# Attention finish with one normalizer tile for four query tiles and one broadcast scaling; the filler's merges queued at once

## The chip, the cores and the metric

The kernel runs on one core of one Trainium2 chip. Five kinds of work are told apart in its profile: TensorE's matmuls (PE) and weight loads (PEld), VectorE (DVE), ScalarE (ACT), GpSimd (POOL), and SyncE (SP), which issues all DMAs. The metric is the device time of one execution in microseconds. Three runs of the kernel before have a median of 1716.93 us (1715.32 to 1719.83).

## The reference, cut to what matters

One layer over 1024 latent tokens of width 1024 and 256 context tokens: a modulated RMS norm, one wide input projection, and two branches on the same input, a gated linear attention and a differential attention. The second one is what the change touches. It has 8 heads; each head's queries and keys come as two components of 64.

```python
def one_block(qs):
    qb1, qb2 = qs
    s1 = jnp.einsum('bhqd,bhkd->bhqk', qb1, k1).astype(jnp.float32) * scale
    s2 = jnp.einsum('bhqd,bhkd->bhqk', qb2, k2).astype(jnp.float32) * scale
    a = jax.nn.softmax(s1, axis=-1) - lam * jax.nn.softmax(s2, axis=-1)
    return jnp.einsum('bhqk,bhkv->bhqv', a.astype(v.dtype), v)
...
b = merge_heads(rms_norm(o_diff) * diff_gain * (1 - lam_init)) * jax.nn.silu(diff_gate)
y = jax.nn.sigmoid(m_gla) * (a @ w_br_gla) + jax.nn.sigmoid(m_diff) * (b @ w_br_diff)
return y @ w_out
```

The output of a head is normalized by its own root mean square. That is why the kernel never divides by the softmax's sum: it forms E0 - lam (z0/z1) E1, where E are the exponentials and z their row sums, and corrects in the norm, whose epsilon is then multiplied by z0 squared: (mean of squares + eps z0^2)^-0.5.

## The kernel before, in words

**How the order of work is set.** The program is written by tasks, Python generators that emit instructions. A planner, class `Driver` (line 57), runs them: it keeps a model of when each engine will be free (`free`), when each tile will be ready (`ready`), and when and by whom it was last used (`last`), all under the tile's name (`key`, lines 82 to 88), so slices of one tile share one record. Every emitted instruction moves these times by its modelled cost (`op`, line 107; the costs are in `Engine`, line 201). A task yields what it waits for, and is resumed by due time and priority, the smallest number first. `d.when(tiles)` (line 90) resumes it 1 us (`AHEAD`) before the tiles are planned to be ready. `d.on(engine, tiles)` (line 96), or `On(t, engine)`, also puts it off as long as that engine is planned to be busy for more than 1 us (`SLACK`) from now; in the meantime tasks with a smaller number may put more work on that engine. What comes out is one fixed order of instructions for each engine. On the chip each engine runs its own queue in that order and waits by semaphores for the data.

**The stages.** Up to about 1000 us the kernel projects and does the linear attention. From about 1000 to 1515 us it runs the differential attention, with other matmuls, the filler, put in between. Then come the rest of the filler and the output projection (`phase_c`).

**Differential attention.** `att_scores` (line 1922) loops over 8 heads and 8 query tiles of 128, 64 units. A unit's scores for both components lie in one PSUM tensor, s5. `att_max` (1966) takes negated row maxima on VectorE (two reductions over 1024 columns, one over the two tails), `att_exp` (1981) takes the exponential on ScalarE and adds it up into z with `accum_out`, `att_mix` (1995) forms the factor from z on VectorE (a reciprocal and a small product) and mixes the two E on VectorE, one instruction over 1280 columns with two SBUF inputs. `att_tr` (2016) transposes E on TensorE, `att_split` (2093) splits the result into a high and a low part, mostly on ScalarE (tile ac) and GpSimd (tiles at4 and at2, "at" in the profile), and `att_av` (2054) multiplies with the values for two units at a time. Each unit has its own small tile z of [128, 2], from the pool of small tiles sm.

**The finish.** `att_ot` (2122) copies an output [128, 256] off PSUM; after every second pair, that is four query tiles, it starts `att_fin` (2133), 16 times in all. This

- loads the gate g [128, 4, 128] (tile b1k),
- forms z2 = eps z0^2, four VectorE instructions of one column, one for each tile's z (line 2142),
- transposes the output back on TensorE, takes its squares on ScalarE with four sums ss, and multiplies by the gate on VectorE, out of PSUM,
- forms ss/128 + z2 with four VectorE instructions of one column (2159), and its power -0.5 on GpSimd,
- scales the gated output by it, four VectorE instructions of 128 columns with a per-partition scalar (2163),
- transposes the result, splits it, and stores it to d_bT.

In the profile these are `sm<-sm` (z2), a part of `sm<-sm,sm` (ss; the others are the minima in `att_max`), `b1k<-b,b1k` (gate) and `b1k<-b1k,sm` (scaling).

**The filler.** `fill` (2181) runs other matmuls at the lowest priority: eight tiles of the gates' projection, then the linear attention's output projection (kind 1) and the differential one's (kind 2). Within attention it has one PSUM buffer, mb; behind the attention's scores it uses mc. `half_tile` (2232) emits 24 matmuls into it and then starts `post` (2219): for kind 1 this merges on VectorE, (m + 1) times the product, into the tile ft, frees the PSUM buffer and stores ft to d_y. There are 16 such merges. `post` has priority -1; those of attention have -2 and -3.

Of the kernel before, what the change touches and what calls it, by code (L numbers as in the profile page):

```python
# [13 lines left out]
ALU = mybir.AluOpType  # L14
# [5 lines left out]
P = 128  # L20
# [5 lines left out]
EPS = 1e-6  # L26
# [219 lines left out]
class Hybrid:  # L246
# [1675 lines left out]
    def att_scores(self):  # L1922

        nc, d = self.nc, self.d
        yield self.ev_b
        s5 = self.t("s5", [P, 2 * T])
        for hd in range(8):
            for qt in range(8):
                pr, qs = qt // 2, slice((qt % 2) * P, (qt % 2) * P + P)
                yield self.ev_k[hd]  # L1930
                yield self.ev_q[hd, pr]
                K, Q = self.K[hd], self.Q[hd, pr]

                def score(po, comp, o, n):
                    bank = po.offset % (2 * T) // 512
                    for j in range(2):
                        e = self.mm(po, Q[comp][:, j, qs], K[comp][:, o:o + n], j == 0, j == 1)
                        self.banked(self.ins, "PE", bank)
                    return e

                u = dict(hd=hd, qt=qt, E=[None, None], mt=self.t("sm", [P, 2]), mx=[self.t("sm", [P, 1]) for _ in range(2)],
                         z=self.t("sm", [P, 2]), left=2, min=[], ev=[Event() for _ in range(3)])

                for comp in range(2):
                    yield from self.acq(f"s{comp}")
                    pm = s5[:, 1536 * comp:1536 * comp + 1024]
                    for x, (o, n) in enumerate(self.MAIN[comp]):
                        e = score(pm[:, x * 512:(x + 1) * 512], comp, o, n)
                        if x == 0:
                            yield AtPE(0)  # L1950
                    d.spawn(self.att_max(u, comp, s5, pm, 3 * comp, 3 * comp + 1), On(e, "DVE"), prio=-3)
                    yield AtPE(0)
                    if comp == 0:
                        yield from self.acq("st")
                        pt = s5[:, 1024:1536].rearrange("p (c k) -> p c k", c=2)
                        for x in range(2):
                            e = score(pt[:, x], x, *self.TAIL[x])
                        d.spawn(self.att_max(u, 2, s5, pt, 2), On(e, "DVE"), prio=-3)
                    elif qt == 7:
                        self.rel("kk", e, 2)  # L1960
                    yield AtPE(0)
                if qt % 2 == 1:
                    self.rel("aq", e, 2)
                d.set(self.ev_u[8 * hd + qt])
# [30 lines left out]
    def att_mix(self, u):  # L1995
        d = self.d
        x = u["qt"] % 2
        cf = self.t("sm", [P, 1])
        E, z = u["E"], u["z"]
        self.dve.reciprocal(cf, z[:, 1:2])  # L2000
        yield On(self.dve.tensor_scalar(cf, cf, z[:, 0:1], self.nlam, ALU.mult, ALU.mult), "DVE")
        if x in self.PC:
            self.pool.tensor_scalar(E[1], E[1], cf, 0.0, ALU.mult, ALU.add)
            e = self.pool.tensor_tensor(E[0], E[0], E[1], ALU.add)
        else:
            e = self.dve.scalar_tensor_tensor(E[0], E[1], cf, E[0], ALU.mult, ALU.add)
        self.att[u["hd"], u["qt"]] = (E[0], z)
        self.rel("e5", e)
        d.set(self.ev_a[u["hd"], u["qt"]], e)

# [111 lines left out]
    def att_ot(self, hd, pr, po):  # L2122

        yield from self.acq("ot")
        ot = self.t("ot", [P, 256])
        e = self.act.activation(ot, po, AF.Copy)
        self.rel(self.PO, e)
        self.ots.append(ot)
        if pr % 2:
            ots, self.ots = self.ots, []  # L2130
            self.d.spawn(self.att_fin(hd, pr // 2, ots, [self.att[hd, 4 * (pr // 2) + x][1] for x in range(4)]), AtPE(e), prio=self.PF)

    def att_fin(self, hd, qd, ots, zs):

        d = self.d
        yield from self.acq("b1k")
        g = self.t("b1k", [P, 4, P])
        self.dma(g, self.d_dg[hd // 4][qd * 512:(qd + 1) * 512, (hd % 4) * P:(hd % 4 + 1) * P].rearrange(
            "(c p) e -> p c e", p=P))
        z2 = self.t("sm", [P, 4])  # L2140
        for x in range(4):
            self.dve.tensor_scalar(z2[:, x:x + 1], zs[x][:, 0:1], zs[x][:, 0:1], EPS, ALU.mult, ALU.mult)
        yield from self.acq("b1k")
        yield from self.acq("b1")
        pt = self.t("b1", [P, 4, P])
        for x in range(4):
            e = self.tr(pt[:, x], ots[x // 2][:, x % 2 * P:x % 2 * P + P])
        self.rel("ot", e, 2)
        yield On(e, "ACT")
        oo = self.t("b1k", [P, 4, P])  # L2150
        ss = self.t("sm", [P, 4])
        for x in range(4):
            e = self.act.activation(oo[:, x], pt[:, x], AF.Square, accum_out=ss[:, x:x + 1])
        yield On(max(e, d.when(g)), "DVE")
        e2 = self.dve.tensor_tensor(g, pt, g, ALU.mult)
        self.rel("b1", max(e, e2))
        yield On(e, "DVE")
        for x in range(4):
            self.dve.tensor_scalar(ss[:, x:x + 1], ss[:, x:x + 1], 1.0 / P, z2[:, x:x + 1], ALU.mult, ALU.add)
        yield d.on("POOL", ss)  # L2160
        yield On(self.pool.tensor_tensor(ss, ss, self.nhalf[:, 0:4], ALU.pow), "DVE")
        for x in range(4):
            e = self.dve.tensor_scalar(oo[:, x], g[:, x], ss[:, x:x + 1], None, ALU.mult)
        self.rel("b1k", e)
        yield AtPE(e)
        yield from self.acq("b1k", 2)
        yield from self.acq("b1")
        pb = self.t("b1", [P, 4, P])
        for x in range(4):
            e = self.tr(pb[:, x], oo[:, x])  # L2170
        self.rel("b1k", e)
        yield On(e, "ACT")
        hi = self.t("b1k", [P, 4, P], F32R)
        lo = self.t("b1k", [P, 4, P], F32R)
        e = yield from self.split2(pb, hi, lo, "b1", self.SF)
        self.store([(self.d_bT[j][hd][:, qd * 512:(qd + 1) * 512], b.rearrange("p x t -> p (x t)")) for j, b in
                    enumerate((hi, lo))], ("b1k", 2), ("fin", 1), ev=self.ev_bT[hd] if qd else None)
        if (hd, qd) == (7, 1):
            self.d.set(self.ev_att)

    def fill(self):


        d, a = self.d, self.a
# [34 lines left out]
        def post(tg, kind, s, half, pm, mt):  # L2219
            cs = slice(half * 512, (half + 1) * 512)  # L2220
            if kind == 0:
                yield from self.acq("ft")
                mt = self.t("ft", [P, 512])
                yield On(0, "ACT")
                self.rel(tg, self.act.activation(mt, pm, AF.Tanh, scale=0.5))
                self.store([(self.d_m[s // 8][s % 8][:, cs], mt)], ("ft", 1))
            else:
                yield d.on("DVE", mt)
                self.rel(tg, self.dve.scalar_tensor_tensor(mt, mt, 1.0, pm, ALU.add, ALU.mult))
                self.store([(self.d_y[s][:, cs], mt)], ("ft", 1))  # L2230

# [51 lines left out]
        while n < len(todo):  # L2283
# [8 lines left out]
            for half in range(2):  # L2292
                for x in two:
                    if i >= 3:
                        yield pace(i)
                    e = yield from half_tile(x, half, rhs)
# [327 lines left out]
```

## Time and profile before

| | us |
|---|---|
| median of 3 runs | 1716.93 |
| the profiled execution | 1718.92 |
| its span, first to last instruction | 1717.2 |
| TensorE busy (matmuls) | 1650.2 |
| VectorE busy | 1220.5 |
| ScalarE busy | 806.9 |
| GpSimd busy | 681.0 |

An engine's busy time counts each moment once, though instructions may overlap in the pipeline; a group's mean is of single instructions. "out<-in" names tiles without their numbers. Most instructions carry line 211, 353 or 379, those of the helpers that emit them, so groups are told apart by their tiles. The granted clock is 0.987 of full speed on average. A timeline row gives start, length, engine, line, operation, tiles, form and count, and in brackets the engine's idle time before it with what ended that.

### The profile page before, as it was taken

The numbers are of one execution on the slowest core, as the hardware profiler recorded it, in microseconds if no ns is written. First come the engines' busy times: TensorE is split into PE (matmuls) and PEld (weight loads), VectorE is DVE, ScalarE is ACT, GpSimd is POOL, SyncE is SP. The second block draws the span as 40 slices with busy tenths as digits, with TensorE's granted clock in tenths as the row PEclk, the third lists the DMA queues.
The fourth block names the chain that finished last, engine by engine and source line by source line (L and its number), as shares of the span: only waits on it lengthen the run. The fifth ranks groups of instructions, "written<-read, shape, count | busy, mean of one in ns | idle before, by whom it ended". The sixth has DMA issues, their size and how long they took to land.

```text
span 1717.2 us, 24802 instructions
## 1 busy us (share of the span) xinstructions
PE 1650.2 (96%) x8381; PEld 1362.1 (79%) x8381; DVE 1220.5 (71%) x2070; ACT 806.9 (47%) x1609; POOL 681.0 (40%) x682
## 2 busy tenths in 40 slices
PE   7899999999999999999999899999999999999999
PEld 3687887887788878788888677888887888887887
DVE  4773976865935375767776679888989878735694
ACT  4784555454432344343332356665666656511231
POOL 1600552562200013335453535667667667720000
PEclk9999999999999999999999999999999999999999
DMA  8537545653334474458999734434576543359521
GB/s 305 195 134 244 167 145 173 195 161 118 114 115 145 153 240 141 141 178 278 278 306 310 208 97 123 129 111 118 156 231 190 154 130 103 94 188 352 164 99 74
DMA packets 267535, 298.68 MB, mean 174 GB/s; under 512 B 23656, under 2 KB 186384, under 8 KB 267408
## 3 DMA queue, kind: packets, MB, share of 16 engines
q1 hardware_dynamic: 267408, 297.10, 55.5%
q8 instruction: 66, 1.08, 0.3%
q14 instruction: 61, 0.50, 0.1%
HBM read 196.89 MB, written 100.14 MB: 173 GB/s over the span
## 4 chain that ended last, share of the span: by engine, by line
PE 66%; DVE 16%; ACT 5%; DMA 4%; issue 4%; POOL 3%; SPq 0%; ACTq 0%; DVEq 0%; POOLq 0%
PE mm L353 17%; PE ma L353 9%; PE mc L353 8%; DVE sm L211 5%; PE gs L353 5%; PE s L353 5%; PE mb L353 5%; PE b L353 4%; PE go L353 4%; PE gt L353 3%; DVE e L211 3%; PE b L379 2%; ACT e L211 2%; PE tp L353 2%; PE tp L379 1%
## 5 line engine op out<-in xcount | busy, mean ns | idle before, releaser
L211 ACT ACTIVATE e<-s,sm 128x1280 f32<-128x1280 f32 x128 | 170.3, 1331 | 125.8 <-DVE sm L211 105.6
L353 PE MATMUL mm<-w,h 128*128 128x512 f32 x864 | 216.4, 400 | 2.8 <-DVE gb L211 1.9
L211 DVE TENSOR_REDUCE sm<-s 128x1 f32<-128x1024 f32 (+1 forms) x192 | 197.2, 1037 | 27.5 <-PE s L353 25.1
L211 POOL TENSOR_TENSOR at<-ac,at 128x512 fp32r<-128x512 f32 x128 | 188.0, 1469 | 10.7
L353 PE MATMUL s<-kk,aq 128*128 128x512 f32 (+1 forms) x768 | 180.0, 369 | 12.5 <-ACT e L211 12.1
L353 PEld LDWEIGHTS mm<-w,h 128*128 128x128 f32 x864 | 160.6, 189 | 37.7 <-DVE gb L211 2.7
L353 PE MATMUL mb<-h,wt 128*128 128x512 f32 x624 | 172.2, 410 | 6.1 <-DVE wt L211 2.9
L211 POOL TENSOR_SCALAR at<-ac 128x512 fp32r<-128x512 f32 x128 | 112.8, 881 | 155.1 <-ACT ac L211 136.0
L353 PEld LDWEIGHTS s<-kk,aq 128*128 128x128 f32 x768 | 122.5, 192 | 38.2 <-ACT e L211 22.9
L353 PE MATMUL mm<-h,w 128*128 128x512 f32 x576 | 144.4, 401 | 3.2 <-DVE w L211 2.0
L353 PEld LDWEIGHTS mb<-h,wt 128*128 128x128 f32 x624 | 111.9, 192 | 26.2 <-DVE wt L211 3.3
L353 PEld LDWEIGHTS mm<-h,w 128*128 128x128 f32 x576 | 108.0, 192 | 28.0 <-DVE w L211 3.7
L353 PE MATMUL b<-at,vv 128*128 128x256 f32 x960 | 128.3, 282 | 1.0 <-DVE at L211 0.9
L211 DVE TENSOR_TENSOR w<-raw,w 128x512 fp32r<-128x512 f32 x110 | 84.1, 791 | 60.9 <-ACT w L211 60.7
L353 PEld LDWEIGHTS b<-at,vv 128*128 128x128 f32 x960 | 121.1, 188 | 6.0 <-POOL at L211 1.3
L353 PE MATMUL mc<-h,wt 128*128 128x512 f32 x528 | 123.2, 393 | 1.4 <-DVE wt L211 0.9
L353 PEld LDWEIGHTS mc<-h,wt 128*128 128x128 f32 x528 | 98.5, 188 | 24.7 <-DVE wt L211 1.8
L211 DVE SCALAR_TENSOR_TENSOR e<-e,sm,e 128x1280 f32<-128x1280 f32 x64 | 114.8, 1794 | 1.2
L211 ACT ACTIVATE ac<-b 128x512 f32<-128x512 f32 x137 | 81.5, 600 | 58.2 <-PE b L379 46.6
L211 POOL TENSOR_TENSOR sm<-sm,nhalf 128x8 f32<-128x8 f32 (+3 forms) x78 | 100.9, 1293 | 18.9 <-DVE sm L211 13.7
L353 PE MATMUL ma<-w,h 128*128 128x512 f32 x384 | 95.9, 395 | 0.4 <-DVE gp L211 0.4
L379 PE MATMUL b<-ident,e 128*128 128x128 f32 x604 | 88.9, 277 | 7.4 <-ACT ac L211 4.5
(377 smaller groups left out, 3184.2 us busy)
## 6 DMA issues: line engine op xcount, KB each, us to landing
raw<-in_w_in SPq DMA_DIRECT2D x40, 512.0 KB, 5.0
rb<-in_w_in SPq DMA_DIRECT2D x64, 256.0 KB, 2.9
aq<-d_qT SPq DMA_DIRECT2D x128, 128.0 KB, 3.9
d_kT<-pl SPq DMA_DIRECT2D x40, 256.0 KB, 2.4
d_dv<-pl SPq DMA_DIRECT2D x40, 256.0 KB, 2.1
kk<-d_kT SPq DMA_DIRECT2D x32, 320.0 KB, 5.0
gv<-d_v SPq DMA_DIRECT2D x40, 256.0 KB, 4.3
vv<-d_dv SPq DMA_DIRECT2D x16, 640.0 KB, 6.2
```

The costliest lines, as they stand in the source:

```text
L211: self.ins = f(out, *args, **kw).ins
L353: self.ins = self.nc.tensor.matmul(out, lhsT, rhs, start=start, stop=stop, skip_group_check=more).ins
L379: self.nc.tensor.transpose(out, src, self.ident[:n, :n])
```

## The change

The four units of a finish get one tile zs [128, 4, 2] in place of four tiles z, and each unit's z is a slice of it. By that, z2 and ss become one instruction each over four columns, where there were four; both of these read two SBUF operands in place of one and per-partition scalars. The scaling becomes one product over 512 columns with ss as a broadcast operand, where there were four of 128 columns. Ahead of it the task also yields until ss and g are planned to be ready. Apart from that, the filler's merge yields `d.when(mt)` in place of `d.on("DVE", mt)`: it is emitted once the planner is within 1 us of the end of its matmuls and of the landing of mt, whatever VectorE has booked.

```diff
+                if qt % 4 == 0:
+                    self.zs = self.t("sm", [P, 4, 2])
                 u = dict(hd=hd, qt=qt, E=[None, None], mt=self.t("sm", [P, 2]), mx=[self.t("sm", [P, 1]) for _ in range(2)],
-                         z=self.t("sm", [P, 2]), left=2, min=[], ev=[Event() for _ in range(3)])
+                         z=self.zs[:, qt % 4], zs=self.zs, left=2, min=[], ev=[Event() for _ in range(3)])
...
-        self.att[u["hd"], u["qt"]] = (E[0], z)
+        self.att[u["hd"], u["qt"]] = (E[0], u["zs"])
...
-            self.d.spawn(self.att_fin(hd, pr // 2, ots, [self.att[hd, 4 * (pr // 2) + x][1] for x in range(4)]), AtPE(e), prio=self.PF)
+            self.d.spawn(self.att_fin(hd, pr // 2, ots, self.att[hd, 2 * pr][1]), AtPE(e), prio=self.PF)
...
-        for x in range(4):
-            self.dve.tensor_scalar(z2[:, x:x + 1], zs[x][:, 0:1], zs[x][:, 0:1], EPS, ALU.mult, ALU.mult)
+        self.dve.scalar_tensor_tensor(z2, zs[:, :, 0], EPS, zs[:, :, 0], ALU.mult, ALU.mult)
...
-        for x in range(4):
-            self.dve.tensor_scalar(ss[:, x:x + 1], ss[:, x:x + 1], 1.0 / P, z2[:, x:x + 1], ALU.mult, ALU.add)
+        self.dve.scalar_tensor_tensor(ss, ss, 1.0 / P, z2, ALU.mult, ALU.add)
         yield d.on("POOL", ss)
         yield On(self.pool.tensor_tensor(ss, ss, self.nhalf[:, 0:4], ALU.pow), "DVE")
-        for x in range(4):
-            e = self.dve.tensor_scalar(oo[:, x], g[:, x], ss[:, x:x + 1], None, ALU.mult)
+        yield d.when(ss, g)
+        e = self.dve.tensor_tensor(oo, g, ss.unsqueeze(2).to_broadcast([P, 4, P]), ALU.mult)
...
-                yield d.on("DVE", mt)
+                yield d.when(mt)
                 self.rel(tg, self.dve.scalar_tensor_tensor(mt, mt, 1.0, pm, ALU.add, ALU.mult))
                 self.store([(self.d_y[s][:, cs], mt)], ("ft", 1))
```

## The prediction

> **What bounds the kernel now.** I read the page first, then the busy time by stretches, then the chain and the waits of the stretch in which attention runs (1000 to 1515 us), then its VectorE instructions by form, and last the timeline around single finishes and merges.
>
> ```profile
> PE 1650.2 (96%) x8381; PEld 1362.1 (79%) x8381; DVE 1220.5 (71%) x2070; ACT 806.9 (47%) x1609; POOL 681.0 (40%) x682
> ```
> ```profile
> 1000.00:1515.00 515.00, 493.11 (x3050) 424.36 (x3049) 438.27 (x757) 312.37 (x605) 350.07 (x301) 0.99 0.47 133
> ```
> ```profile
> 1360.00:1380.00 20.00, 17.10 (x95) 14.73 (x95) 14.83 (x30) 10.56 (x24) 11.52 (x12) 0.83 0.42 129
> ```
> ```profile
> by line: DVE sm L211 16.7%; PE s L353 15.7%; PE b L353 13.7%; DVE e L211 11.0%; PE mb L353 10.9%; PE b L379 7.2%; issue 7.0%; ACT e L211 6.6%; DVE b1k L211 3.2%; DVE wt L211 1.0%; ACT ac L211 0.9%; POOL at L211 0.8%; PE mc L379 0.8%; DVE at
> ```
> ```profile
> ACT e L211 <- DVE sm L211: 96.6, 49, 5.7
> ...
> PE s L353 <- ACT e L211: 9.7, 20, 2.0
> ```
>
> TensorE sets the time: 96% busy. Work that is taken off VectorE can only shorten the time in which TensorE stands still or runs below its clock. In the attention stretch (columns: length, then PE, PEld, DVE, ACT, POOL busy, PE clock) TensorE is idle for 515.0 - 493.1 = 21.9 us. The reader is to see in the chain that a third of this stretch passes through VectorE (sm, e, b1k, wt), although VectorE is only 438.3 / 515 = 85% busy: a score matmul waits for the exponential to free its PSUM half, and that one waits for the row maximum on VectorE (96.6 us in 49 waits). So VectorE time is worth something here, but at most those 21.9 us, plus what the clock loses: 0.83 over 1360 to 1380 is 0.17 x 20 = 3.4 us.
>
> **The change part by part.** VectorE's rows of the same stretch:
>
> ```profile
> L211 DVE TENSOR_REDUCE sm<-s 128x1 f32<-128x1024 f32 x125 | 152.1, 1216 | 17.0 <-PE s L353 16.2 <-PE b L379 0.2
> L211 DVE SCALAR_TENSOR_TENSOR e<-e,sm,e 128x1280 f32<-128x1280 f32 x64 | 114.8, 1794 | 1.2
> L211 DVE TENSOR_REDUCE sm<-s 128x2 f32<-128x512 f32 x63 | 42.8, 679 | 0.8 <-PE s L353 0.8
> L211 DVE TENSOR_SCALAR sm<-sm,sm 128x1 f32<-128x1 f32 x186 | 35.3, 210 | 4.5
> ...
> L211 DVE TENSOR_SCALAR sm<-sm,sm,nlam 128x1 f32<-128x1 f32 x63 | 17.2, 273 | 2.3
> L211 DVE TENSOR_TENSOR b1k<-b,b1k 128x512 f32<-128x512 f32 x15 | 10.2, 680 | 1.3 <-issue 1.3
> L211 DVE RECIPROCAL sm<-sm 128x1 f32<-128x1 f32 x63 | 10.0, 158 | 27.0 <-ACT e L211 27.0
> L211 DVE TENSOR_SCALAR sm<-sm 128x1 f32<-128x1 f32 x64 | 9.1, 203 | 0.0
> ```
> and of the whole run, the scaling and two forms near to what the change adds:
> ```profile
> L211 DVE TENSOR_SCALAR b1k<-b1k,sm 128x128 f32<-128x128 f32 x64 | 26.8, 480 | 6.7 <-POOL sm L211 6.7
> ...
> L211 DVE TENSOR_TENSOR p<-p,sm 128x512 f32<-128x512 f32 x15 | 10.4, 692 | 14.8 <-POOL sm L211 14.8
> ...
> L211 DVE TENSOR_TENSOR gkk<-gk,gx 128x128 f32<-128x128 f32 x26 | 7.4, 288 | 0.0
> ```
>
> *The scaling.* Four instructions become one in each of 16 finishes. Now they cost 26.8 / 16 = 1.67 us a finish. The new one multiplies 512 columns by a broadcast operand; p<-p,sm (line 1452) is exactly that form, 692 ns, so the broadcast itself costs nothing that can be seen beside it.
>
> Why are the old ones at 480 ns on average? Because of GpSimd:
>
> ```profile
> L211 DVE SCALAR_TENSOR_TENSOR e<-e,sm,e x64: 1539/1612/2579, 1000.2 to 1491.9; 128x1280 f32<-128x1280 f32 x64
> L211 DVE TENSOR_SCALAR sm<-sm x64: 197/204/208, 1040.2 to 1511.0; 128x1 f32<-128x1 f32 x64
> L211 DVE TENSOR_SCALAR b1k<-b1k,sm x64: 273/280/1327, 1053.0 to 1521.3; 128x128 f32<-128x128 f32 x64
> ```
> ```profile
> L211 POOL TENSOR_TENSOR at<-ac,at x128: 1263/1294/2601, 1005.9 to 1509.5; 128x512 fp32r<-128x512 f32 x128
> ```
> ```profile
> 1030.82 1.30 POOL L211 TENSOR_TENSOR at<-ac,at 128x512 fp32r<-128x512 f32 x1
> 1030.93 2.54 DVE L211 SCALAR_TENSOR_TENSOR e<-e,sm,e 128x1280 f32<-128x1280 f32 x1
> ```
>
> The mix at 1030.93 started 0.11 us behind a GpSimd instruction that ended 1.19 us later, and took 2.54 us where the shortest took 1.54: it stood still behind it. A scaling's 273 ns becomes 1327 in the same way. The [128 x 1] instructions are never caught (197 to 208). An instruction with two SBUF inputs waits, by the mix's mean against its minimum, (1794 - 1539) = 0.255 us on average. So the new scaling costs 0.692 + 0.255 = 0.95 us and saves 0.72 x 16 = 11.6 us of VectorE. It has one chance to be caught where there were four.
>
> *The two small groups* (z2 and ss): four become one, twice in each finish. Four cost 9.1 / 16 = 0.57 us (z2's row; ss lies in the row of 186 at the same 210 ns). The new ones have four columns and two SBUF inputs. No row shows that; from 692 ns at 512 columns and 288 at 128 the slope is 1.05 ns, so 288 - 124 x 1.05 = 0.158 us alone (an estimate). Unlike the old they can be caught; I add the mix's 0.255 and get 0.41, a saving of 0.16 x 32 = 5.1 us. Bounds: never caught, 13.2 us; always behind a whole 1294 ns instruction, (0.158 + 1.294 - 0.57) x 32 = 28 us lost.
>
> The Trainium skill (SBUF — State Buffer, section Who interferes with whom) states it as a rule: an instruction of VectorE with at most one SBUF input, outside its two-port modes, does not contend with GpSimd, while one with two SBUF inputs does, and whoever comes second is blocked for the whole of the other's instruction. It speaks against the two small merges; the rows agree with it for the mix, and no row here shows four columns. By that rule alone, with the wait as long as the mix's, the sum stays as it is; the rival below takes it to its end.
>
> *From VectorE time to the end.* The chain holds 16.7% x 515 = 86 us of the 266.5 us that the sm rows add up to (152.1 + 42.8 + 35.3 + 17.2 + 10.0 + 9.1), or 0.32, and 3.2% x 515 = 16.5 of b1k's 26.8 + 10.2 = 37.0, or 0.45. So 11.6 x 0.45 + 5.1 x 0.32 = 6.9 us lie on it. What is late next is the exponential on ScalarE (6.6% of the chain) and TensorE's own queue, whose order is fixed; I count half, 3.4 us. The choice has no row; the ends are 0 and 6.9.
>
> *The merges.* 16 of them (ten on PSUM tile mb within attention, six on mc behind it) no longer wait until the planner sees VectorE less than 1 us booked; each goes to its queue as soon as its matmuls are within 1 us of their planned end. One place shows what the old rule did:
>
> ```profile
> 1356.88 1.63 PE L353 MATMUL mb<-h,wt 128*128 128x512 f32 x6
> ...
> 1371.19 0.68 DVE L211 SCALAR_TENSOR_TENSOR ft<-ft,mb 128x512 f32<-128x512 f32 x1
> ```
> ```profile
> 1371.92 1.65 PE L353 MATMUL mb<-h,wt 128*128 128x512 f32 x3 [2.57 <-DVE ft L211]
> ```
> ```profile
> L318 SPq DMA_DIRECT2D d_y<-ft x16: 319/334/1311, 1321.8 to 1563.9; - x16
> ...
> PE mb L353: 3.3, 2
> ```
>
> The tile was full at 1358.51, the merge began at 1371.19, and TensorE stood 2.57 us for the only mb buffer, and then ran at the lower clock (3.4 us lost, above): 6.0 us at one place, of 3.3 us of matmul waits for ft in all. Since everything behind the first finish is laid out anew, that place may go while another one comes: I count half, 3.0 us. A merge put ahead costs those queued behind it (row maxima, mixes, which the exponentials await) its 0.68 us each, but adds no work: ten in attention, 6.8 us at worst if each were waited for, less than nothing if TensorE had filler instead. The store to d_y that each merge issues moves up in the SP queue with it, 0.33 us of issue each, past loads of aq and b1k; the transfer is the same, and I cost it at nothing, at most 16 x 0.33 = 5 us of that queue.
>
> *The shared normalizer tile.* Is there a new wait between the four tiles? On the chip waits go by slices of a tile:
>
> ```profile
> 1157.24 2.50 DVE L211 TENSOR_SCALAR b1k<-b1k,sm 128x128 f32<-128x128 f32 x4
> ```
> ```profile
> 1159.09 0.35 PEld L379 LDWEIGHTS b<-ident,b1k 128*128 128x128 f32 x3
> 1159.79 0.14 PEld L379 LDWEIGHTS b<-ident,b1k 128*128 128x128 f32 x1 [0.34 <-DVE b1k L211]
> ```
>
> Three transposes started before the fourth scaling had ended at 1159.74; only the fourth waited. So the chip gets no such wait, but the planner does: it keeps its times by tile name (lines 82 to 88), so it will think that an exponential which adds into a shared tile must follow the mix before it. That changes orders, not work. I cost it at 0, with the bounds of the third rival.
>
> Sum: 3.4 + 3.0 = 6.4 us. The profiled execution had a span of 1717.2 and took 1718.92, so 1712.5 for it; the median of the runs, 1716.93, lies 2.0 lower, and by that the forecast is **1710.5 us**. A measurement of this kernel tells apart about 0.3%, 5.2 us: faster is below 1711.8, slower above 1722.1.
>
> **The rivals.** *All of it counts*: 6.9 on the chain and 6.0 at the merges, nothing late next: 1704.0. For: VectorE is a third of the chain. Against: 21.9 us of idle in all are to be won, spread over many causes.
>
> *Hidden*: TensorE's queue is in order and full, the freed VectorE time becomes idle time, and half of the merge's place remains: about -2, 1715. It is also what comes out if the merges were mostly queued at once already (the six behind attention have an idle VectorE).
>
> *GpSimd's lock, slower*: place, the z2 and ss instructions and the scaling; price, a wait of w each. VectorE time changes by 13.2 + 16 x (1.67 - 0.69) - 48 w = 28.9 - 48 w, so it decides at w = 0.60 us. At w = 1.29, a whole GpSimd instruction, the chain grows by 32 x 0.88 x 0.32 + 16 x 0.31 x 0.45 = 11.2 us, less the merges' 3: 1725. Against it stands the mix's 0.255.
>
> *The planner's false order, slower*: three of four units share a tile with an earlier one, 48 exponentials. If each of half of them slips behind one ScalarE copy, of 80.9 / 136 = 0.60 us, and TensorE waits for it, 24 x 0.60 = 14.4 us come and 6.4 go: 1725. It decides from 11 such slips, where the gain is gone.
>
> ```profile
> L211 ACT ACTIVATE ac<-b 128x512 f32<-128x512 f32 x136 | 80.9, 600 | 54.4 <-PE b L379 42.8 <-POOL at L211 9.9 <-POOL b1k L211 1.6
> ```
>
> **How the numbers follow.** Forecast 0.45 (0.38 of it below 1711.8), all of it 0.12, hidden 0.23, the lock 0.08, the false order 0.12. Faster 0.50, same 0.30, slower 0.20. The range is 1702 to 1722: it leaves out the lock, most of the false order and the low end of the second case.
>
> **What would show it.** In the profile after: 16 b1k<-b1k,sm instructions of 128x512 near 0.95 us on average; 32 small ones near 0.41, at times above 1; fewer than 438 us of VectorE in attention; no mb wait of over 2 us for ft; no exponential queued later. I am wrong if the small ones average above 0.6, or if TensorE's idle time in attention is not below 21.9 us though VectorE's fell by some 17.

## The result, and the profile after

The changed kernel takes 1707.71 us (median of 4 runs, 1707.46 to 1708.47) against 1717.61 us before (4 runs). The ratio is 0.994, 95% interval 0.9921 to 0.9958, so the change makes the kernel faster by 9.9 us by the medians. The profiled execution took 1707.85 us with a span of 1705.8. The forecast was 1710.5, a gain of 6.4.

The engines of the page after:

```profile
PE 1644.7 (96%) x8381; PEld 1359.1 (80%) x8381; DVE 1197.1 (70%) x1926; ACT 807.0 (47%) x1609; POOL 680.6 (40%) x682
```

VectorE has 144 instructions fewer, as 16 finishes with three groups of three fewer should give. Attention does not end at the same time any more, so a window with fixed ends would compare different work. The following rows go from the start of the first exponential to the end of the last one, and from there to the end; the columns are length, then busy time (and instructions) of PE, PEld, DVE, ACT and POOL, the granted clock, and the share and rate of the DMAs. First the kernel before:

```profile
995.00:1490.70 495.70, 472.23 (x2891) 404.79 (x2892) 431.56 (x737) 306.86 (x588) 329.89 (x282) 0.99 0.48 135
1490.70:1717.20 226.50, 221.47 (x1035) 182.66 (x1033) 131.86 (x214) 53.37 (x99) 23.12 (x23) 1.00 0.51 171
```

and the changed kernel:

```profile
996.70:1483.00 486.30, 469.38 (x2907) 404.41 (x2908) 413.65 (x612) 306.16 (x586) 322.12 (x280) 1.00 0.49 140
1483.00:1705.80 222.80, 217.44 (x1019) 179.59 (x1017) 128.34 (x195) 54.02 (x101) 26.27 (x24) 1.00 0.50 169
```

Attention is 9.4 us shorter and what follows it 3.7 us. That is more than the 9.9 us of the medians: the stretch ahead of attention, which the change does not touch, was 1.7 us longer in this execution (996.7 against 995.0), and the profiled execution of before lies 1.3 us above its median. VectorE is busy for 17.9 us less in attention; TensorE's idle time there falls from 495.7 - 472.2 = 23.5 to 16.9 us. What stood at the place of the late merge, 1360 to 1380 us, now reads

```profile
1360.00:1380.00 20.00, 18.33 (x125) 16.09 (x124) 17.95 (x27) 11.62 (x25) 16.41 (x14) 1.00 0.50 146
```

with the full clock in place of 0.83. The chain of 1000 to 1515 us has changed hands:

```profile
by line: PE s L353 19.7%; PE b L353 14.9%; PE mb L353 14.4%; DVE sm L211 11.6%; PE b L379 9.1%; DVE e L211 6.9%; ACT e L211 5.5%; issue 4.6%; POOL at L211 2.7%; PE mc L353 2.0%; ACT ac L211 1.3%; DMA b1k<-d_dg 1.3%; DVE b1k L211 1.3%; POOL 
```

VectorE's sm, e and b1k had 30.9% of it and have 19.8%; the matmuls of s, b and mb took the rest over. The waits of the same stretch that answer to those shown of before:

```profile
ACT e L211 <- DVE sm L211: 82.3, 51, 4.1
...
PE s L353 <- ACT e L211: 5.5, 14, 1.1
...
PE mb L353 <- DVE ft L211: 1.3, 1, 1.3
```

The new instructions, by form over the whole run, and then by tile with minimum, median and maximum in ns:

```profile
L211 DVE TENSOR_TENSOR b1k<-b1k,sm 128x512 f32<-128x512 f32 x16 | 16.3, 1020 | 11.2 <-POOL sm L211 11.1
...
L211 DVE SCALAR_TENSOR_TENSOR sm<-sm 128x4 f32<-128x4 f32 x16 | 6.0, 374 | 0.0
L211 DVE SCALAR_TENSOR_TENSOR sm<-sm,sm 128x4 f32<-128x4 f32 x16 | 4.8, 299 | 0.0
```
```profile
L211 DVE TENSOR_TENSOR b1k<-b1k,sm x16: 682/897/1780, 1054.3 to 1516.7; 128x512 f32<-128x512 f32 x16
```
```profile
L211 DVE SCALAR_TENSOR_TENSOR sm<-sm x16: 145/239/1253, 1041.8 to 1505.1; 128x4 f32<-128x4 f32 x16
L211 DVE SCALAR_TENSOR_TENSOR sm<-sm,sm x16: 151/152/989, 1048.0 to 1514.5; 128x4 f32<-128x4 f32 x16
```

A broadcast operand costs hardly anything beside the work itself: 682 ns at the least, where a product of the same shape without one (p<-h,h, in the kernel before) takes 675 to 678. And four columns are held up by GpSimd as 512 are: 145 ns alone, 1253 at the worst. One of them, 0.15 us of work, shows it: it starts 0.31 us behind a GpSimd instruction and ends with it, at 1048.9.

```profile
1047.64 1.28 POOL L211 TENSOR_TENSOR at<-ac,at 128x512 fp32r<-128x512 f32 x1
...
1047.95 0.99 DVE L211 SCALAR_TENSOR_TENSOR sm<-sm,sm 128x4 f32<-128x4 f32 x1
```

### The profile page after: what moved, and what is told of

Its sections match the earlier page's. It is cut to its first block, busy times and chain, and to the rows that moved or that the text cites. A ratio compares the mean times of both kernels' runs of the same rounds, so it can differ in the third digit from the quotient of the medians.

```text
span 1705.8 us, 24642 instructions
## 1 busy us (share of the span) xinstructions
PE 1644.7 (96%) x8381; PEld 1359.1 (80%) x8381; DVE 1197.1 (70%) x1926; ACT 807.0 (47%) x1609; POOL 680.6 (40%) x682
## 4 chain that ended last, share of the span: by engine, by line
PE 70%; DVE 14%; ACT 5%; POOL 4%; issue 4%; DMA 3%; SPq 0%; ACTq 0%; DVEq 0%; POOLq 0%
PE mm L353 16%; PE mc L353 9%; PE ma L353 8%; PE s L353 6%; PE mb L353 6%; PE gs L353 5%; PE b L353 4%; DVE sm L211 4%; PE go L353 4%; PE gt L353 4%; PE b L379 3%; PE tp L353 2%; DVE e L211 2%; ACT e L211 2%; POOL sm L211 2%
## 5 line engine op out<-in xcount | busy, mean ns | idle before, releaser
L211 POOL TENSOR_SCALAR at<-ac 128x512 fp32r<-128x512 f32 x128 | 101.7, 794 | 152.0 <-ACT ac L211 139.5
L211 DVE SCALAR_TENSOR_TENSOR e<-e,sm,e 128x1280 f32<-128x1280 f32 x64 | 111.3, 1739 | 1.1
```

The costliest lines, as they stand in the source:

```text
L211: self.ins = f(out, *args, **kw).ins
```

## The experiments

Two things change at once in this kernel, and they are easily taken for one. The chip has fewer VectorE instructions to run, and the planner, which books other costs and emits the merges earlier, lays out other queues for all engines. To part them, some of the kernels below let the planner book one form of the finish and issue the other. Then every queue keeps its order (in `order_old_ops_new` and `order_old_small_new` SyncE's alone differs, by one store of ft that stands one place earlier), and only the instructions in VectorE's slots change. Gains are given as ratios to the kernel before with their intervals; 0.001 is 1.7 us.

**New finish in the old queues.** `order_old_ops_new` starts from the kernel before:

```diff
+        self.dve.emits = False                        # book only
         for x in range(4):
             self.dve.tensor_scalar(z2[:, x:x + 1], zs[x][:, 0:1], zs[x][:, 0:1], EPS, ALU.mult, ALU.mult)
+        self.dve.emits, self.dve.plan = True, False   # issue only
+        self.dve.scalar_tensor_tensor(z2, zt[:, :, 0], EPS, zt[:, :, 0], ALU.mult, ALU.mult)
+        self.dve.plan = True
```

and so for ss and the scaling; z is a slice of one tile zt, with a record for each slice.

> The queues of TensorE, ScalarE and GpSimd are those of the kernel before, entry by entry; the planner still books four instructions for each group, but one is issued (z2, ss, scaling) out of the shared tile, and the merges wait as before. Theory A, VectorE's freed time itself brings the gain whatever the order: most of the 9.9 us, that is 6 to 10 us below before. Theory B, the gain comes from the other order that the planner lays out when it books less: 0 to 3 us below before, with the half-clock stalls near 1371 and 1473 still there. My forecast had 3.4 us for this part.

Measured 0.9954 (0.9941 to 0.9967), 7.9 us faster. Its attention and what follows:

```profile
997.60:1483.50 485.90, 467.60 (x2894) 403.93 (x2894) 412.14 (x611) 306.13 (x588) 335.01 (x282) 0.99 0.49 138
1483.50:1709.90 226.40, 220.71 (x1032) 182.17 (x1030) 129.72 (x196) 53.34 (x99) 23.39 (x23) 1.00 0.51 171
```

Attention is shorter by 9.8 us, the rest is as long as before. And the late merge still stops TensorE, since its place in the queue is the old one:

```profile
1368.71 1.66 PE L363 MATMUL mb<-h,wt 128*128 128x512 f32 x6 [2.57 <-DVE ft L215]
```

Freed VectorE time is theory A, and it brings 7.9 us without any help from the order. Of the 9.8 us between the two traces, 5.2 are idle time of TensorE (23.5 to 18.3) and 4.6 are busy time for as many matmuls, which fits the clock: after this stall of 2.57 us six matmuls took 1.66 us, in the kernel before, after a stall of the same length, three took 1.65. So the low clock is no fixed price of that stall.

**Old finish in the new queues.** `order_new_ops_old` does the reverse on the changed kernel: the new forms are booked, the old fours are issued.

> The queues of TensorE, ScalarE and GpSimd are those of the changed kernel; the planner books one instruction for each group, but the old four are issued in its place, so VectorE has some 15 us more to do than in the changed kernel. Theory A: 0 to 4 us below before. Theory B: 6 to 10 us below before, as the changed kernel.

Measured 0.9978 (0.9967 to 0.9988), 3.8 us. That is what order and early merges bring together. It is less than the merges alone bring, by 2.2 us, though the two intervals overlap:

**The merges alone.** `merge_only` is the kernel before with one line changed, `yield d.when(mt)`.

> The kernel before with the merges queued at once, nothing else; everything up to the first merge at about 1310 us stays. If the merges are the cause: 6 us or more below before, since the place at 1371 (2.57 us of stall and 3.4 us of clock) goes. By my forecast 3.0 us below. If they only matter together with the finish: 0 within 2 us.

Measured 0.9965 (0.9951 to 0.9978), 6.0 us. Its attention and what follows:

```profile
994.60:1490.30 495.70, 474.15 (x2919) 406.47 (x2920) 436.32 (x739) 307.01 (x589) 329.77 (x282) 1.00 0.49 138
1490.30:1710.50 220.20, 215.28 (x1008) 177.63 (x1006) 130.23 (x212) 52.89 (x99) 22.34 (x23) 1.00 0.50 171
```

Attention is as long as before to the tenth of a microsecond, but the rest is 6.3 us shorter. TensorE's filler matmuls (those that read wt) in the same two stretches tell why, first of the kernel before, then of this one:

```profile
995.00:1490.70 495.70, 150.70 (x549) 0.99 0.48 135
1490.70:1717.20 226.50, 130.54 (x557) 1.00 0.51 171
```
```profile
994.60:1490.30 495.70, 156.50 (x573) 1.00 0.49 138
1490.30:1710.50 220.20, 124.84 (x531) 1.00 0.50 171
```

The mb buffer comes free sooner: worked out from the timelines, the ten merges on mb start 30.5 us in all behind the end of their matmuls before, and 14.4 us here. So more filler runs in the gaps of attention, and some 25 matmuls fewer are left for the end, 130.54 - 124.84 = 5.7 us. What did not shrink is TensorE's waiting for a merge. It moved to another place (2.16 us at 1357.96); first the kernel before, then this one:

```profile
PE mb L353 <- DVE ft L211: 2.6, 1, 2.6
```
```profile
PE mb L353 <- DVE ft L211: 2.5, 2, 2.2
```

Over both stretches together TensorE is busy for 4.3 us less with as many matmuls (693.7 to 689.4 us), which fits the clock, and idle for 2.0 us less, by other waits.

**The finish alone.** `finish_only` is the changed kernel with `yield d.on("DVE", mt)` as before.

> The changed kernel with the merges waiting as before. Theory A or B: 6 to 10 us below before. If the merges are the cause: no more than 3 us below before. My forecast had 3.4 us for this part.

Measured 0.9976 (0.9967 to 0.9985), 4.1 us. It runs the same instructions as `order_old_ops_new`, with the same rule for the merges, and is 3.8 us slower: only the order differs, and the new bookings led the planner to a worse one. By the timelines its merges on mb start 47.9 us in all behind their matmuls, against 28.2 in `order_old_ops_new`, which may be a part of it.

```profile
995.10:1485.90 490.80, 467.77 (x2894) 401.98 (x2894) 417.30 (x612) 306.61 (x589) 323.30 (x281) 0.99 0.49 138
```

Attention is 4.9 us longer than in `order_old_ops_new`, with TensorE idle for 23.0 us in place of 18.3.

**The sum without that loss.** `order_merge_ops_new` is `order_old_ops_new` with the merges' line changed as well.

> The order that the planner lays out with the old finish booked and the merges queued at once (that of merge_only on TensorE, ScalarE, GpSimd and SyncE), with the new finish's instructions issued in it. If the freed VectorE time (8.0 us in the old order) and the merges (6.0 us) add up: 13 to 15 us below before, some 4 us below the changed kernel. If both win the same idle time twice: 8 to 10 us below before, no better than the changed kernel.

Measured 1704.52 us, 0.992 (0.9907 to 0.9933), 13.7 us: 7.9 and 6.0 add up. This is the fastest kernel of the study, 3.2 us below the changed one by the medians, though the two intervals overlap a little.

```profile
994.60:1483.60 489.00, 472.71 (x2918) 408.30 (x2919) 414.05 (x613) 307.16 (x588) 334.20 (x282) 0.99 0.49 139
1483.60:1703.50 219.90, 215.04 (x1009) 177.75 (x1007) 128.79 (x194) 52.92 (x99) 22.59 (x23) 1.00 0.50 171
```

Both signatures stand side by side: a shorter attention, and a shorter rest.

**The finish in parts, in the old queues.** `order_old_scale_new` issues only the scaling in its new form, `order_old_small_new` only z2 and ss.

> All queues of before, with one broadcast scaling issued in place of four, nothing else. By VectorE time as I forecast it (11.6 of 16.7 us) 70% of the 8.0 us: 5 to 6 us below before. If the scaling's place matters more than its time, because the transposes and the next exponentials wait behind it: 7 to 8 us. If the many small instructions are what costs: under 3 us.

Measured 0.9963 (0.9951 to 0.9976), 6.4 us. That lies between what its time and what its place should bring; the interval does not part the two.

> All queues of before, with z2 and ss as one instruction each out of the shared tile, the scaling in four as before. By VectorE time (5.1 of 16.7 us as forecast; 32 x (0.57 - 0.33) = 7.7 us as the changed kernel's trace has it): 2 to 3.5 us below before. If GpSimd's lock eats it: 0 within 1.5 us, or slower.

Measured 0.997 (0.996 to 0.998), 5.2 us. The small ones bring more than the share of VectorE time that I gave them; GpSimd's lock does not eat them. The two gains sum to 11.6 us and together they gave 7.9. The intervals are too wide to say whether that is an overlap or scatter; it stays open.

**Another order, the same work.** `nudge_up` and `nudge_down` are the kernel before with one line in the finish, which issues nothing:

```diff
+        d.free["DVE"] = d.free["DVE"] + 0.05
```

or minus 0.05; the planner comes upon other queues behind the first finish.

> The kernel before, the same instructions, but the planner books 0.05 us more on VectorE at each of the 16 finishes, 0.8 us in all, so that it lays out another order behind the first finish. It shows what another order alone is worth. If order is noise of several us (the finish's own order cost 4 us in finish_only against order_old_ops_new): 3 us or more off before, either way. If orders are as good as each other: within 2 us of before, and the 4 us are the new bookings' own fault.

Measured 1.0031 (1.0021 to 1.0041), 5.3 us slower.

> The kernel before, the same instructions, with 0.05 us less booked on VectorE at each finish; another order. If nudge_up's 5.3 us were the scatter of orders: anywhere from 5 us faster to 5 us slower, and not the mirror image of nudge_up by any reason. If the order of before stood out as a good one: slower again, by 3 to 6 us.

Measured 1.003 (1.0016 to 1.0044), 5.2 us slower. The two are no mirror images; of the three orders that of before is the best. Attention of `nudge_up` has TensorE idle for 27.9 us, where it was 23.5:

```profile
994.20:1491.00 496.80, 468.90 (x2897) 402.18 (x2898) 425.77 (x739) 306.10 (x588) 331.02 (x282) 0.99 0.47 135
```

This trace shows a part of the loss alone: its execution took 1719.47 us, where the median of `nudge_up` is 1723.76. Some of the loss is likely clock, since the nudged kernels ran at a mean granted clock of 0.9870 and 0.9864, and the kernel before beside them at 0.9878 and 0.9887.

`after_nudge_up15` and `after_nudge_down15` do the same to the changed kernel, with 0.15.

> The changed kernel, the same instructions, with 0.15 us more booked on VectorE at each finish (0.05 leaves every queue as it is). It shows how much of the 9.9 us hangs on the one order that the planner fell upon. If the gain is one of freed time and early merges: 5 us or more below before whatever the order, with a scatter of 3 to 5 us around the changed kernel. If it was that order: 0 to 3 us below before.

Measured 0.9983 (0.9973 to 0.9992), 2.9 us faster than before.

> As after_nudge_up15, with 0.15 us less booked at each finish: a third order for the changed kernel's instructions, with the same two outcomes.

Measured 0.999 (0.9979 to 1.0), 1.7 us, and the interval reaches 1. Both lie in the 0 to 3 us that were expected if the gain was that of one order. So the changed kernel's own order is a lucky one as well: two neighbours of it give back most of the 9.9 us.

```profile
994.50:1492.00 497.50, 473.53 (x2915) 408.77 (x2916) 418.01 (x613) 306.89 (x589) 320.89 (x282) 0.99 0.48 137
1492.00:1713.40 221.40, 216.46 (x1011) 178.85 (x1009) 130.08 (x194) 52.18 (x98) 23.38 (x23) 1.00 0.50 171
```

In `after_nudge_up15` the rest is as short as with the early merges, VectorE is busy for 13.6 us less than before, and yet attention is 11.2 us longer than in the changed kernel: TensorE is idle there for 24.0 us in place of 16.9. Against the nudged kernels of before, at 1.0031 and 1.003, both are still ahead, by some 7 to 8 us: the mean of three orders is 1.0020 with the old instructions and rules, and 0.9971 with the new ones.

One thing goes with these losses. In `finish_only` and the four nudged kernels the merges on mb start 40 to 48 us in all behind their matmuls; in the kernel before, the changed one and all the others it is 12 to 31. No run changes this alone, so it is not shown as the cause.

**One more step.** `best_z2_act` is `order_merge_ops_new` with z2 on ScalarE (only what is issued is shown):

```diff
-        self.dve.scalar_tensor_tensor(z2, zt[:, :, 0], EPS, zt[:, :, 0], ALU.mult, ALU.mult)
+        self.nc.scalar.activation(z2, zt[:, :, 0], AF.Square, scale=EPS ** 0.5)
```

> order_merge_ops_new with z2 formed on ScalarE (one square of four columns with the root of epsilon as its scale) in place of VectorE. VectorE is rid of 16 instructions that GpSimd can hold up, 16 x 0.37 = 6 us as measured in the changed kernel; ScalarE gets 16 of about 0.25 us by its shortest rows. If VectorE time is worth at the end what it was in the finish (8.0 us for some 17): 2 to 3 us below order_merge_ops_new. If the other engines are late by now: within 1.5 us of it, or slower where a square stands ahead of an exponential.

Measured 1705.04 us, 0.9927 (0.9913 to 0.9942), no different from `order_merge_ops_new`. Its trace shows that little was freed: VectorE is busy in attention for 411.88 us against 414.05, 2.2 us less and not 6. At 0.41 us for each microsecond, the rate of `order_old_ops_new` (7.9 us for 431.56 - 412.14 = 19.4), that is 0.9 us, too little to be seen here.

```profile
992.90:1483.70 490.80, 474.63 (x2917) 410.88 (x2918) 411.88 (x599) 308.23 (x603) 333.58 (x282) 0.99 0.49 139
```

## Why the prediction was right, and where its terms were off

The sum was 3.4 + 3.0 + 0 = 6.4 us. The runs say 7.9 + 6.0 - 3.8 = 10.1, against 9.9 measured. VectorE's mechanism was the right one; the merges' gain came in another way than forecast; all three sizes were off, in directions that in part cancel. That the total came so near is luck in part: with the two nudged orders the same edits gave 2.9 and 1.7 us against the kernel before, which by the prediction's 5.2 us would be the same.

*The saving on VectorE.* Forecast 16.7 us. By the rows of the three forms it is 44.8 - 27.1 = 17.7 over the whole run (for ss, the row of 192 instructions held 36.3 us, and that of 128 now holds 27.4). The mixes, which were not touched, cost 3.5 us less as well (114.8 to 111.3), so VectorE's total fell by more, 23.4 us, of which 17.9 in attention. The scaling came out at 1.02 us where 0.95 was forecast, z2 at 0.374 and ss at 0.299 where it was 0.41. The way to the wait, from the mix's mean against its minimum, held: the waits are 0.34, 0.23 and 0.15 us (mean less minimum) where 0.255 was taken.

*From VectorE to the end.* This is the step that failed: "I count half, 3.4 us". The chain's shares alone gave 6.9, and the measured 7.9 (5.7 to 10.1 by its interval) lies at that, not at its half. I halved because ScalarE and TensorE's queue would be next; the chain after speaks for room there, since the exponential's share fell as well, from 6.6 to 5.5%, and its wait for VectorE from 96.6 to 82.3 us. By the chain, a row maximum that comes earlier moves the exponential, the release of PSUM and the score matmul with it; this is read from the chain, and no run moves the maximum alone. About half of it came as less busy time in the traced pair, as by a higher clock, which this step did not count.

*The merges.* Full price 6.0, of which I counted half, 3.0; measured 6.0. That the full price and the measured gain are the same number is chance. The price was 2.57 us of stall and 3.4 of clock at one place; in `merge_only` the stall came back elsewhere (2.5 us of waits for ft in place of 2.6), and what went is 4.3 us of TensorE's busy time, as with a higher clock, and 2.0 us of other idle time. The clock's part was rightly foreseen in kind, the stall's was not. The low clock of 1371 is gone, and what I did not name is that filler moves from the end into attention. In the changed kernel the waits for ft are down to 1.3 us. It still has a late merge, for which TensorE does not stand still, because it had other work until it was due:

```profile
1388.08 0.94 PE L353 MATMUL mb<-h,wt 128*128 128x512 f32 x3
...
1397.14 0.68 DVE L211 SCALAR_TENSOR_TENSOR ft<-ft,mb 128x512 f32<-128x512 f32 x1
...
1398.81 0.47 PE L353 MATMUL mb<-h,wt 128*128 128x512 f32 x1
```

*The order.* I costed the new order at 0 and had it as a rival only through the shared tile's record. It cost 3.8 us by two pairs (`finish_only` against `order_old_ops_new`, the changed kernel against `order_merge_ops_new`) and 2.2 by a third (`order_new_ops_old` against `merge_only`), all at the edge of the noise, and hid a part of the halvings' error in the sum. The reason that I gave for it was wrong: with a record for each slice in place of one for the tile, the planner lays out the same queues for the changed kernel, entry by entry, on all five engines, so the shared record is not what changed the order, and the rival of the false order falls with it. The nudges show that no reason of that kind is needed; 0.05 us booked more or less does as much.

*GpSimd's lock.* It decided at a mean wait of 0.60 us; the three forms' waits average 0.24. This rival was ruled out, though its mechanism is real: the rule of the Trainium skill (SBUF — State Buffer, Who interferes with whom) that a VectorE instruction with two SBUF inputs contends with a GpSimd instruction that reads SBUF agrees with the trace for four columns too, 145 ns alone and 1253 at most, where the old [128 x 1] instructions were never over 218.

*Hidden.* The forecast's 0.23 for no visible change is refuted for the finish by `order_old_ops_new` and for the merges by `merge_only`.

## What to carry to other kernels

Where one fixed order for each engine comes out of a planner, a change has two effects, the work it removes and the order that its new costs bring about; here the second was worth nearly as much as the parts of the first (3.8 us, and over 5 us by a nudge that changes no instruction). To learn what a saving is worth, issue the new instructions in the old order; to learn whether a new time is more than luck, nudge a booked cost and look again. Length of attention and length of the rest, taken between the same two instructions in every run, told the two edits apart in the old queues: freed VectorE time shortens the first, earlier release of the filler's buffer the second. Across orders this does not hold: `after_nudge_up15` has an attention of 497.5 us, longer than before, with VectorE time freed.

## What was not expected of the hardware

The size of the scatter by order alone: with the same instructions, three orders of the kernel before lie at 1, 1.0031 and 1.003, and three of the changed kernel at 0.994, 0.9983 and 0.999. A saving of 19.4 us on an engine that is 87% busy (431.56 of 495.70 us), and is not the bound, gave 7.9 us at the end in the old queues, 0.41 for each microsecond, as the chain's shares had it (6.9 / 16.7). And the same stall of 2.57 us was followed by half the matmul speed in one trace and by the full speed in another.
